# A gated delta net trunk on one core: a pair's small loads and the result stores go to GpSimd's DMA queue, and a pair waits ten steps instead of seven

## The chip, the core and the metric

The kernel runs on one core of a Trainium2 chip. The core has five engines, each with its own instruction queue: TensorE (PE in the profile, its weight loads PEld), VectorE (DVE), ScalarE (ACT), GpSimd (POOL) and SyncE (SP). A transfer between the chip's memory and the core's own memory (a DMA) is issued from the queue of one engine, in that queue's order, and runs on 16 DMA engines. The metric is the device time of one execution in microseconds, as the median of several runs.

## What is computed

A trunk of two layers over 272 tokens (16 learned ones in front of 256) of width 2048: a short convolution and a feed-forward part, then a gated delta net and a feed-forward part. The change touches the gated delta net alone:

```
proj = h @ w_in                                  # q, k (16 heads of 128), v, z (32 heads of 128), b, a
q, k, v = silu(conv4(proj[q, k, v]));  q, k = l2norm(q), l2norm(k)
beta = sigmoid(b);  g = -exp(a_log) * softplus(a + dt_bias)
# per head and chunk of tokens, g summed within the chunk:
decay = exp(g_t - g_s) for s <= t, else 0
T = inverse(I + strict(beta k k^T * decay))
u, w = T (beta v), T (beta k exp(g))
v_new = u - w S;   o = (q exp(g)) S + (q k^T * decay) v_new
S = S * exp(g_last) + (k exp(g_last - g))^T v_new
out = (rmsnorm(o) * silu(z)) @ w_out
```

## The kernel before

All arithmetic is fp32, and a weight product is made of three fp32r products: a weight is split into a high and a low part (`whi` on ScalarE, L107, `wlo` on VectorE, L108), and so are the activations; `mm3` issues the three products, L260 to L262, for each 128x128 block. Weights come in pieces of 512 KB, each by one DMA from SP's queue (L95), three pieces deep, and are split into up to four pieces ahead of use.

The gated delta net is a list of units: the gates, 16 k heads, 16 q heads, 32 z heads, then 32 v heads mixed with 128 output blocks ("o": eight stages of 16 blocks, each stage taking four finished heads). A k, q, z or v unit is 48 products over two pieces of weights; an o block is 12.

Around the units runs a clockwork. `ck.tick()` advances it: four ticks in a k, q, z or v unit and one in an o block, so that 12 weight products lie between two ticks (some o ticks and the ticks of a `drain` have none). `ck.later(n, f)` emits the instructions of `f` n ticks later, `ck.side(gen, rate)` lets a generator emit a step per tick. Since a chain of order-only dependences (`in_program_order`) keeps each engine's queue in the order in which it was emitted, a tick is a place in the program and not a time.

What the change touches:

- `k_post` (L676), `q_post` (L697), `gram` (L789) and `z_post` (L854) store the activated k, q, the Gram matrices and z to scratch in the chip's memory (`Kd`, `Qd`, `KKd`, `Zd`), from SP's queue, between the weight pieces.
- From the Gram matrices and the gates, VectorE makes the inverses of all heads at once (`inverse`), while the z units run. It leaves `Ud` and `Vd` (inverse blocks), `Md` (an off-diagonal block) and before that `Dd` (decay) in the chip's memory, all from GpSimd's queue.
- `pair(j)` works on the two value heads of key head j. It first loads `kh`, `qh` (L866, L868), then by `load` (L876), with one DMA per head: decay `D` and inverse `U` (92 partitions, 3 rows of 92 each), and the blocks `U2`, `M2`, `V2` (46 partitions, 3 rows of 46), then the gate rows `e` (L889). At step 1 it transposes k and multiplies `U2` by `M2` (L895, L900; ScalarE copies `kt` and `Y`); at step 2 `V2` by `Y` (L912) and q by k (L917); then three chunks of three steps each: `r` (L929, L932, L937), `vn` and `vd` (L941, L945, L950), the state and the output (L954 to L971). After the last chunk `tail` and `scale` normalise, load that pair's two `z` tiles (`zl`, L999) and, three ticks later, `back` transposes, multiplies by z into `y` (L1012) and splits the result (L380, L381) for the o blocks.
- `cores` paces the pairs: pair j is loaded when no other waits to start, its step 1 comes `LW` ticks later, at most two pairs are in their chunks, and each of them makes a step every two ticks.
- GpSimd's queue holds at that time the memsets of the v tiles' padding (L1099), which wait for a free buffer, and nothing else.

Of the kernel before, what the change touches and what calls it, by code (L numbers as in the profile page):

```python
# [19 lines left out]


class Dims:
    def __init__(self, D=2048, DFF=5632, NK=16, SEQ=256, META=16, C=92, FS=4, HS=4, PIECE=8, ZE=32, VA=(16, 5, 5, 4, 2, 0, 0, 0), YX=8, VB=11, GRATE=0.7, IRATE=dict(k=.3, q=.6, z=.8, v=.6, o=.6), LW=7, LIVE=2, GAP=2, RB=3, PB=4, CL=4, ZS=1, IL=6, GL=11, GY=3.0, LAG=2, X0=0, X1=4, XR=3, XP=1, FIN=3):
        self.D, self.DFF, self.NK, self.SEQ, self.META, self.C = D, DFF, NK, SEQ, META, C
        self.FS, self.HS, self.PIECE, self.ZE, self.VA, self.YX, self.VB, self.GRATE, self.IRATE = FS, HS, PIECE, ZE, VA, YX, VB, GRATE, IRATE
        self.X0, self.X1, self.XR, self.XP, self.FIN, self.LAG, self.LW, self.LIVE, self.GAP, self.RB, self.PB, self.CL = X0, X1, XR, XP, FIN, LAG, LW, LIVE, GAP, RB, PB, CL
        self.ZS, self.IL, self.GL, self.GY = ZS, IL, GL, GY
        self.T = SEQ + META
        self.KT = D // P
        self.NF = DFF // P  # L30
        self.NV = 2 * NK
        self.N = -(-self.T // C)
        self.TP = self.N * C
        self.FT = self.NF // FS
        self.NST = self.NV // HS
        kt = self.KT
        self.G4 = min(4, NK, self.KT)
        o = 0
        self.off = {}
        for name, w in (("norm", 5 * kt), ("scc", 3 * kt), ("gcc", 4 * (2 * self.NK + self.NV)),  # L40
                        ("gnw", 1), ("alog", 1), ("dtb", 1)):
            self.off[name] = o
            o += w
        self.NPAR = o
# [130 lines left out]
def trunk(ctx: ExitStack, tc: tile.TileContext, d: Dims, xT, par, w_s0, w_sc, w_sco, w_q, w_k, w_v, w_z, w_ba,  # L175
          w_go, w_gu, w_dn, outT):
    nc = tc.nc
    T, KT, NK, NV, C, N, HS = d.T, d.KT, d.NK, d.NV, d.C, d.N, d.HS
# [3 lines left out]
    TP, H = d.TP, C // 2  # L182
    PK = min(d.PIECE, KT)
    G4 = d.G4
    ck = Clockwork()
# [122 lines left out]
    class Norm:  # L308


        def __init__(self, idx, a):
            self.idx, self.a, self.n, self.wait = idx, a, 0, []
            self.acc = tp.tile([P, T], F32, tag="nacc", name="nacc", bufs=1)
# [28 lines left out]
        def finish_last(self):  # L342
# [7 lines left out]
            v = tp.tile([P, nt], F32, tag="lv", name="lv", bufs=1)  # L350
            nc.vector.tensor_scalar(out=v, in0=ps, scalar1=1.0 / d.D, scalar2=EPS, op0=ALU.mult, op1=ALU.add)
            r = tp.tile([P, nt], F32, tag="lr", name="lr", bufs=1)
# [7 lines left out]
        def finish(self):  # L360
# [4 lines left out]
            v = self.acc  # L365
            nc.vector.tensor_scalar(out=v[:, a:T], in0=ps[:, a:T], scalar1=1.0 / d.D, scalar2=EPS,
                                    op0=ALU.mult, op1=ALU.add)
# [49 lines left out]
    with tc.tile_pool(name="scy", bufs=1) as yp, tc.tile_pool(name="sct", bufs=2) as sp:  # L417
# [20 lines left out]
        for g in range(KT // G4):  # L438
            for u, ps in enumerate(pp):
# [7 lines left out]
                for i in range(G4):  # L447
                    k = g * G4 + i
# [90 lines left out]
    def dram(name, shape):  # L539
        return dp.tile(shape, F32, name=name)  # L540

    Gd, Bd, Ed, Ld = dram("Gd", [NV, TP]), dram("Bd", [NV, TP]), dram("Ed", [NV, TP]), dram("Ld", [NV, N])
    Kd, Qd = dram("Kd", [NK, P, TP]), dram("Qd", [NK, P, TP])
    Ekd, rkd, rqd = dram("Ekd", [NV, TP]), dram("rkd", [NK, TP]), dram("rqd", [NK, TP])
    KKd = dram("KKd", [NK * N, CC])
    Dd, Ud = dram("Dd", [NI, CC]), dram("Ud", [NI, CC])
    Md, Vd = dram("Md", [NI, H * H]), dram("Vd", [NI, H * H])
    Zd = dram("Zd", [NV, P, S])
# [11 lines left out]
    def psc():  # L560
        return pc_.tile([P, 512], F32, tag="c", name="psc")

    def psd():
        return pd_.tile([P, 512], F32, tag="d", name="psd")
# [104 lines left out]
    def k_post(j, ps):  # L669
        cv = conv_in(ps, vc, NK + j)  # L670
        kr = kt_.tile([P, TP], F32, tag="kr", name="kr", bufs=4)
        nc.gpsimd.memset(kr[:, T:TP], 0.0)

        def act():
            nc.scalar.activation(out=kr[:, :T], in_=cv, func=AF.Silu)
            ck.later(2, lambda: nc.sync.dma_start(out=Kd[j], in_=kr))  # L676

        ck.later(d.CL, act)
        ck.later(d.GL, lambda: gram(j, kr))
# [4 lines left out]
    def q_post(j, ps):  # L684
        if j == 0:
            state["qs"] = psd()
        qs = state["qs"]
        cv = conv_in(ps, vc, j, QA)
        qr = kt_.tile([P, TP], F32, tag="qr", name="qr")
        nc.gpsimd.memset(qr[:, :M0], 0.0)  # L690
        nc.gpsimd.memset(qr[:, T:TP], 0.0)
        sq = kt_.tile([P, T], F32, tag="sq", name="sq")

        def act():
            nc.scalar.activation(out=qr[:, M0:T], in_=cv[:, M0:T], func=AF.Silu)
            nc.scalar.activation(out=sq, in_=qr[:, :T], func=AF.Square)
            ck.later(2, lambda: nc.sync.dma_start(out=Qd[j], in_=qr))  # L697

        ck.later(d.CL, act)

        def ss():
            nc.tensor.matmul(qs[:NK, :T], onehot[:, NK - 1 - j:2 * NK - 1 - j], sq, start=(j == 0),
                             stop=(j == NK - 1))
            if j == NK - 1:
                ck.side(q_norm(qs), 1.0)

        ck.later(8, ss)
# [72 lines left out]
    def gram(j, raw):  # L780
        pk = psc()
        for n in range(N):
            kc = raw[:, n * C:(n + 1) * C]
            nc.tensor.matmul(pk[:C, n * C:(n + 1) * C], kc, kc, start=True, stop=True)
        kk = kt_.tile([C, N, C], F32, tag="kk", name="kk")
        nc.scalar.copy(out=kk.rearrange("s n c -> s (n c)"), in_=pk[:C, :N * C])

        def store():
            nc.sync.dma_start(out=KKd[j * N:(j + 1) * N].rearrange("n (s c) -> s n c", s=C), in_=kk)  # L789
            if j == NK - 1:  # L790
                ck.side(when_gates_done(), 1.0)

        ck.later(1, store)

    def when_gates_done():
        while not state.get("gdone"):
            yield 1.0
        yield from load_w()
# [51 lines left out]
    def z_post(j, ps):  # L850
        z = vc.tile([P, S], F32, tag="cx", name="z")
        nc.vector.tensor_tensor(out=z, in0=ps, in1=Rt[:, M0:T], op=ALU.mult)
        ck.later(d.ZS, lambda: nc.scalar.activation(out=z, in_=z, func=AF.Silu))
        ck.later(d.ZS + 2, lambda: nc.sync.dma_start(out=Zd[j], in_=z))  # L854


    vts = {}
# [5 lines left out]
    def pair(j, vp):  # L863
# [7 lines left out]
        def load(tag, src, a, b, bufs, r=slice(None), c=slice(None)):  # L871

            t = vp.tile([a, 2, N, b], F32, tag=tag, name=tag, bufs=bufs)
            for e in range(2):
                g = e * NK + j
                nc.sync.dma_start(out=t[:, e], in_=src[g * N:(g + 1) * N].rearrange(  # L876
                    "n (s c) -> s n c", c=(C if src.shape[1] == CC else H))[r, :, c])
            return t

        D = load("D", Dd, C, C, 3)  # L880
        U = load("U", Ud, C, C, 3)
        hi = slice(H, C)
        U2, M2, V2 = load("U2", Ud, H, H, 1, hi, hi), load("M2", Md, H, H, 1), load("V2", Vd, H, H, 1)
        qg, kg = [], []
        for x, xd in ((qg, Ed), (kg, Ekd)):
            t = vp.tile([P, 2, TP], F32, tag="e", name="e", bufs=6)
            for e in range(2):
                g = e * NK + j
# [16 lines left out]
        for x, y in ((qg, qh), (kg, kh)):  # L905
            nc.vector.tensor_tensor(out=x, in0=x, in1=y[:, None, :].to_broadcast([P, 2, TP]), op=ALU.mult)
        nc.vector.tensor_tensor(out=kd, in0=D[:, :, :, C - 1], in1=rkt[:, None, JN].to_broadcast([C, 2, N]),
                                op=ALU.mult)
        yield
        pu = psd()  # L910
        for i in range(2 * N):
            nc.tensor.matmul(pu[:H, i * H:(i + 1) * H], V2[:, i // N, i % N], Y[:, i * H:(i + 1) * H], start=True,  # L912
                             stop=True)
        nc.scalar.copy(out=U[:H, :, :, H:], in_=pu[:H, :2 * N * H].rearrange("s (e n c) -> s e n c", e=2, n=N))
        pq = psc()
# [8 lines left out]
        for n in range(N):  # L924
# [15 lines left out]
            for e in range(2):  # L940
                nc.tensor.matmul(pv[:C, e * P:(e + 1) * P], U[:, e, n], r[:, e * P:(e + 1) * P], start=True,  # L941
                                 stop=True)
# [36 lines left out]
        z = []  # L979
# [11 lines left out]
        def scale(steps, ro):  # L991
            for _ in steps:
                pass
            for i in range(2 * N):
                x = ot[:, i // N, i % N]
                nc.scalar.activation(out=x, in_=x, func=AF.Copy, scale=ro[:, i:i + 1])  # L996
            for e in range(2):
                z.append(vp.tile([P, S], F32, tag="zl", name="zl", bufs=2))
                nc.sync.dma_start(out=z[e], in_=Zd[2 * j + e])  # L999
            ck.later(3, lambda: back(0))  # L1000

        def back(e):
# [52 lines left out]
    for kind, j in gseq:  # L1055
# [8 lines left out]
        if kind == "o":  # L1064
            s, jj = divmod(j, KT)
# [17 lines left out]
        if kind == "z":  # L1083
            ps = psum(S)
            gemm(ps, xs, KT, M0, T)
            z_post(j, ps)
            ck.tick()
            continue
# [121 lines left out]
```

## Time and profile before

| | us |
|---|---|
| median of 3 runs (3059.32 to 3062.54) | 3061.09 |
| the profiled execution | 3066.19 |
| its span | 3064.4 |
| TensorE busy, share of the span | 2919.6, 95% |
| VectorE, ScalarE, GpSimd busy | 1789.2, 1368.4, 178.0 |
| mean granted clock of TensorE, share of full speed | 0.975 |
| data moved | 539.52 MB at 176 GB/s |

In the profile a wait is written as "engine line <- what released it". A row of the stretches gives, for each engine, the microseconds in which it was busy and its number of instructions, then the granted clock of TensorE as a share of full speed (its two levels are 1.2 and 2.4 GHz, so 0.5 and 1.0, and a stretch shows their mix), the busy share of the DMA engines and the rate. The units of v and o, the pairs with them, run from about 1660 to 2256 us; the gates, k, q and z before them from about 1210.

### The profile page before, as it was taken

How to read it: one execution, taken by the hardware profiler on the slowest of the kernel's cores; microseconds unless marked ns; L12 is line 12 of the kernel's file. 1: busy time of each engine (PE TensorE's matmuls, PEld its weight loads, DVE VectorE, ACT ScalarE, POOL GpSimd, SP SyncE). 2: the span in 40 equal slices, each digit the busy share in tenths (PEclk: the TensorE clock that was granted, in tenths of full speed). 3: DMA queues.
4: the chain of work that ended last, by engine and by line, in shares of the span. 5: the costliest groups of instructions: out<-in, count | busy, mean ns of one | idle time of the engine just before them, and what ended most of it. 6: DMA issues, size and time to landing. Idle time of an engine off the chain costs nothing. (4 is left out here: it accounts for less than half of the span.)

```text
span 3064.4 us, 57534 instructions
## 1 busy us (share of the span) xinstructions
PE 2919.6 (95%) x23501; PEld 2878.4 (94%) x23501; DVE 1789.2 (58%) x2628; ACT 1368.4 (45%) x2218; POOL 178.0 (6%) x306
## 2 busy tenths in 40 slices
PE   9999999999999999899998888988899999999998
PEld 8999999999999999888988788887899999999997
DVE  6555555555555557758885455555576555555555
ACT  5333444433434345745334455545454444444434
POOL 2000100000000001201000000000010000000001
PEclk9999999999999999999999899999999999999999
DMA  6555555556555565687556545444455555556564
GB/s 199 190 176 169 179 174 172 178 167 186 173 169 186 164 175 179 182 240 220 183 180 200 148 142 154 137 156 133 154 162 180 188 190 176 193 176 198 186 177 151
DMA packets 212696, 539.52 MB, mean 176 GB/s; under 512 B 55664, under 2 KB 82624, under 8 KB 211952
## 3 DMA queue, kind: packets, MB, share of 16 engines
q1 hardware_dynamic: 208144, 517.92, 54.5%
q0 software_dynamic: 2480, 15.01, 1.8%
q8 instruction: 184, 3.01, 0.4%
q10 hardware_dynamic: 1808, 2.92, 0.3%
q14 instruction: 80, 0.66, 0.1%
HBM read 515.03 MB, written 20.74 MB: 175 GB/s over the span
## 5 line engine op out<-in xcount | busy, mean ns | idle before, releaser
L108 DVE TENSOR_TENSOR wlo<-raw,whi 128x1024 fp32r<-128x1024 f32 (+2 forms) x995 | 1125.1, 1140 | 838.3 <-ACT whi L107 835.1
L262 PE MATMUL mm<-xh,wlo 128*128 128x272 f32 (+2 forms) x5136 | 1481.0, 288 | 20.9 <-DVE wlo L108 20.7
L260 PE MATMUL mm<-xh,whi 128*128 128x272 f32 (+2 forms) x5136 | 1485.4, 289 | 15.8 <-ACT whi L107 15.8
L261 PE MATMUL mm<-xl,whi 128*128 128x272 f32 (+2 forms) x5136 | 1476.3, 287 | 0.8 <-DVE xl L326 0.8
L107 ACT CAST whi<-raw 128x1024 fp32r<-128x1024 f32 (+2 forms) x995 | 962.4, 975 | 534.9 <-PE mm L261 329.9
L262 PEld LDWEIGHTS mm<-xh,wlo 128*128 128x128 f32 x5136 | 977.5, 190 | 29.1 <-DVE wlo L108 28.5
L260 PEld LDWEIGHTS mm<-xh,whi 128*128 128x128 f32 x5136 | 980.9, 191 | 25.0 <-ACT whi L107 16.8
L261 PEld LDWEIGHTS mm<-xl,whi 128*128 128x128 f32 x5136 | 978.0, 190 | 1.7 <-DVE xl L326 1.6
L262 PE MATMUL mm<-ah,wlo 128*128 128x272 f32 (+1 forms) x1408 | 399.3, 284 | 0.0
L261 PE MATMUL mm<-al,whi 128*128 128x272 f32 (+1 forms) x1408 | 399.0, 283 | 0.0
L260 PE MATMUL mm<-ah,whi 128*128 128x272 f32 (+1 forms) x1408 | 398.6, 283 | 0.0
L260 PEld LDWEIGHTS mm<-ah,whi 128*128 128x128 f32 x1408 | 265.1, 188 | 0.0
L261 PEld LDWEIGHTS mm<-al,whi 128*128 128x128 f32 x1408 | 264.6, 188 | 0.0
L262 PEld LDWEIGHTS mm<-ah,wlo 128*128 128x128 f32 x1408 | 264.3, 188 | 0.0
L380 ACT CAST ah<-u 128x272 fp32r<-128x272 f32 (+1 forms) x88 | 36.4, 413 | 286.5 <-POOL u L508 286.5
L260 PE MATMUL mm<-yh,whi 128*128 128x256 f32 x512 | 154.3, 301 | 9.3 <-DVE h L467 9.3
L261 PE MATMUL mm<-yl,whi 128*128 128x256 f32 x512 | 148.0, 289 | 0.0
L262 PE MATMUL mm<-yh,wlo 128*128 128x256 f32 x512 | 147.8, 289 | 0.0
L508 POOL TENSOR_TENSOR u<-u,g 128x272 f32<-128x272 f32 (+1 forms) x88 | 66.4, 754 | 1223.4 <-DVE u L507 1223.4
L520 ACT ACTIVATE g<-g 128x272 f32<-128x272 f32 (+1 forms) x88 | 37.3, 424 | 214.6 <-DVE g L519 214.6
L467 DVE TENSOR_TENSOR h<-mm,h 128x256 f32<-128x256 f32 (+1 forms) x272 | 113.1, 425 | 28.7 <-PE mm L262 26.4
L575 DVE SCALAR_TENSOR_TENSOR cc<-cx,prm,cc 128x271 f32<-128x271 f32 (+5 forms) x192 | 95.4, 497 | 40.0 <-ACT cc L571 35.0
(325 smaller groups left out, 2156.5 us busy)
## 6 DMA issues: line engine op xcount, KB each, us to landing
raw<-w_gu SPq DMA_DIRECT2D x352, 512.0 KB
raw<-w_dn SPq DMA_DIRECT2D x128, 384.0 KB
raw<-w_sc SPq DMA_DIRECT2D x84, 512.0 KB
raw<-w_dn SPq DMA_DIRECT2D x128, 320.0 KB
raw<-w_z SPq DMA_DIRECT2D x64, 512.0 KB
raw<-w_v SPq DMA_DIRECT2D x64, 512.0 KB
raw<-w_go SPq DMA_DIRECT2D x64, 512.0 KB
raw<-w_sco SPq DMA_DIRECT2D x32, 512.0 KB
```

Source lines behind the costliest of these rows:

```text
L107: self.nc.scalar.copy(out=hi[:, s], in_=t[:, s])
L108: self.nc.vector.tensor_tensor(out=lo[:, s], in0=t[:, s], in1=hi[:, s].bitcast(F32), op=ALU.subtract)
L260: nc.tensor.matmul(ps, wh, x[0][:, a:b], start=start, stop=False)
L261: nc.tensor.matmul(ps, wh, x[1][:, a:b], start=False, stop=False)
L262: nc.tensor.matmul(ps, wl, x[0][:, a:b], start=False, stop=stop)
L380: nc.scalar.copy(out=hi, in_=x)
L467: nc.vector.tensor_tensor(out=h[j][:, a:T], in0=ps, in1=h[j][:, a:T], op=ALU.add)
L508: nc.gpsimd.tensor_tensor(out=u1, in0=u1, in1=g1, op=ALU.mult)
L520: nc.scalar.activation(out=g1, in_=g1, func=AF.Silu)
L575: nc.vector.scalar_tensor_tensor(out=cv[:, a + i:T], in0=x1[:, a:T - i], scalar=pcol("gcc", 4 * ci + 3 - i), in1=cv[:, a + i:T], op0=ALU.m ...
```

## The change

- `load` issues from GpSimd's queue instead of SP's, so that a pair's ten loads of `D`, `U`, `U2`, `M2` and `V2` leave SP's queue; `kh`, `qh` and the gate rows `e` stay on SP.
- Those ten are put into another order: `U2`, `M2` (step 1), `D`, then `V2` and `U` (step 2).
- The stores `Kd`, `Qd`, `KKd`, `Zd` and the loads `zl` go to GpSimd's queue as well.
- `LW`, the ticks between a pair's loads and its step 1, is 10 instead of 7. It has no part in how far ahead the weights are loaded.

```diff
-... IL=..., LW=7, LIVE=2, GAP=2, ...
+... IL=..., LW=10, LIVE=2, GAP=2, ...
...
-            ck.later(2, lambda: nc.sync.dma_start(out=Kd[j], in_=kr))
+            ck.later(2, lambda: nc.gpsimd.dma_start(out=Kd[j], in_=kr))
...
-            ck.later(2, lambda: nc.sync.dma_start(out=Qd[j], in_=qr))
+            ck.later(2, lambda: nc.gpsimd.dma_start(out=Qd[j], in_=qr))
...
-            nc.sync.dma_start(out=KKd[j * N:(j + 1) * N].rearrange("n (s c) -> s n c", s=C), in_=kk)
+            nc.gpsimd.dma_start(out=KKd[j * N:(j + 1) * N].rearrange("n (s c) -> s n c", s=C), in_=kk)
...
-        ck.later(d.ZS + 2, lambda: nc.sync.dma_start(out=Zd[j], in_=z))
+        ck.later(d.ZS + 2, lambda: nc.gpsimd.dma_start(out=Zd[j], in_=z))
...
-                nc.sync.dma_start(out=t[:, e], in_=src[g * N:(g + 1) * N].rearrange(
+                nc.gpsimd.dma_start(out=t[:, e], in_=src[g * N:(g + 1) * N].rearrange(
                     "n (s c) -> s n c", c=(C if src.shape[1] == CC else H))[r, :, c])
...
+        hi = slice(H, C)
+        U2, M2 = load("U2", Ud, H, H, 1, hi, hi), load("M2", Md, H, H, 1)
         D = load("D", Dd, C, C, 3)
+        V2 = load("V2", Vd, H, H, 1)
         U = load("U", Ud, C, C, 3)
-        hi = slice(H, C)
-        U2, M2, V2 = load("U2", Ud, H, H, 1, hi, hi), load("M2", Md, H, H, 1), load("V2", Vd, H, H, 1)
...
-                nc.sync.dma_start(out=z[e], in_=Zd[2 * j + e])
+                nc.gpsimd.dma_start(out=z[e], in_=Zd[2 * j + e])
```

SP's queue at the loads of the sixth pair, among v and o units, before (`raw` is a piece of weights, `U_...`, `M_...`, `V_...` are the 46-row blocks; "x2" is one DMA for each head):

```order
L95 DMA raw_19836<-w_v 128x1024
L866 DMA kh<-Kd 128x276
L868 DMA qh<-Qd 128x276
L876 DMA D<-Dd 92x3x92 x2
L876 DMA U<-Ud 92x3x92 x2
L876 DMA U_19868<-Ud 46x3x46 x2
L876 DMA M_19871<-Md 46x3x46 x2
L876 DMA V_19874<-Vd 46x3x46 x2
L889 DMA e<-Ed 128x276 x2
L889 DMA e<-Ekd 128x276 x2
L999 DMA zl<-Zd 128x256 x2
L95 DMA raw_19938<-w_v 128x1024
```

and SP's queue at the loads of one pair in the changed kernel:

```order
L95 DMA raw_20481<-w_v 128x1024
L866 DMA kh<-Kd 128x276
L868 DMA qh<-Qd 128x276
L890 DMA e<-Ed 128x276 x2
L890 DMA e<-Ekd 128x276 x2
L95 DMA raw_20558<-w_v 128x1024
```

Eighteen DMAs between two pieces of weights have become six. GpSimd's queue among the v and o units, where before there stood the memsets alone, in the changed kernel:

```order
L1000 DMA zl<-Zd 128x256 x2
L1100 MEMSET vt 128x4
L876 DMA U_19709<-Ud 46x3x46 x2
L876 DMA M_19712<-Md 46x3x46 x2
L876 DMA D<-Dd 92x3x92 x2
L876 DMA V_19718<-Vd 46x3x46 x2
L876 DMA U<-Ud 92x3x92 x2
L1100 MEMSET vt 128x4 x2
L1000 DMA zl<-Zd 128x256 x2
```

The ten loads of a pair now stand ahead of the `zl` loads of an older pair. TensorE's queue at a pair's step 1 among o blocks, before:

```order
L262 MATMUL mm<-yh,wlo_20203 128x256
L895 MATMUL psc<-ident,kh 92x128 x2
L900 MATMUL psd<-U_20231,M_20234 46x46 x6
L968 MATMUL psc<-S,e 92x128
L969 MATMUL psc<-vn,D 92x128
L968 MATMUL psc<-S,e 92x128
L969 MATMUL psc<-vn,D 92x128
L929 MATMUL psc<-ident,vt 92x128
L932 MATMUL psc<-S,e 92x128
L929 MATMUL psc<-ident,vt 92x128
L932 MATMUL psc<-S,e 92x128
L260 MATMUL mm<-yh,whi_20293 128x256
```

and in the changed kernel, at a pair's step 1 (its lines are one higher):

```order
L262 MATMUL mm<-xh_90,wlo_20606 128x272
L896 MATMUL psc<-ident,kh 92x128 x2
L901 MATMUL psd<-U_20529,M_20532 46x46 x6
L260 MATMUL mm<-xh_92,whi_20657 128x272
L261 MATMUL mm<-xl_93,whi_20657 128x272
```

The steps of the two older pairs no longer share the tick of step 1; they stand in other ticks. Over the whole program the pairs are loaded every 10 ticks before (with longer pauses towards the end) and every 13 now, the sixteenth at the 206th instead of the 195th tick after the first v unit's start. Of the 256 ticks of v and o units the changed program has one drain: the last o stage waits for the last pair, whose `y` is emitted eight ticks after its last chunk, and only four o blocks are left to stand in between.

## Rows read from the trace of the kernel before

**Rows 1.** Busy time by stretch, us from the span's start; columns in its first row.

```profile
core 0: us, PE busy (x) PEld busy (x) DVE busy (x) ACT busy (x) POOL busy (x), PEclk, DMA share, GB/s
...
1215.00:1350.00 135.00, 124.13 (x966) 121.57 (x965) 99.07 (x142) 86.67 (x119) 19.46 (x38) 0.95 0.72 216
1350.00:1470.00 120.00, 110.18 (x819) 100.64 (x818) 84.88 (x137) 53.00 (x78) 18.39 (x60) 0.96 0.79 218
1470.00:1660.00 190.00, 168.95 (x1313) 161.02 (x1312) 145.13 (x170) 65.72 (x84) 2.35 (x14) 0.97 0.58 180
1660.00:2256.00 596.00, 520.94 (x4160) 502.89 (x4160) 332.14 (x724) 305.24 (x801) 2.29 (x26) 0.91 0.49 149
2062.00:2110.00 48.00, 45.99 (x385) 44.23 (x383) 29.05 (x68) 29.95 (x84) 0.00 (x0) 1.00 0.46 143
```

**Rows 2.** The page's chain that ended last: shares of the span, by engine, by line.

```profile
PE 34%; DMA 3%; SPq 3%; DVE 2%; ACT 2%; issue 1%; DVEq 0%; ACTq 0%
PE mm L260 10%; PE mm L262 10%; PE mm L261 10%; SPq L876 2%; DMA raw<-w_v 1%; DMA zl<-Zd 1%; SPq L889 1%; DVE wlo L108 1%; ACT whi L107 1%; PE psc L969 0%; PE psc L968 0%; PE psd L941 0%; ACT ot L996 0%; DMA raw<-w_go 0%; DVE h L467 0%
```

**Rows 3.** The same chain around one pair: start, us, what.

```profile
1806.86 3.27 DMA zl<-Zd
1810.22 0.49 DVE y L1012
...
1812.81 0.38 ACT vn L945
1813.23 1.19 PE psd L900 x12
```

**Rows 4.** SP's queue at one pair: start, us, line, DMA.

```profile
1792.41 0.38 SPq L866 DMA_DIRECT2D kh<-Kd  x1
...
1794.31 6.53 SPq L876 DMA_DIRECT2D U<-Ud  x4
...
1806.86 0.90 SPq L999 DMA_DIRECT2D zl<-Zd  x2
1807.87 0.38 SPq L95 DMA_DIRECT2D raw<-w_v  x1
```

**Rows 5.** Waits from 1660 to 2256: total us, times, longest.

```profile
ACT whi L107 <- DMA raw<-w_v: 46.2, 10, 13.2
...
DVE y L1012 <- DMA zl<-Zd: 36.4, 8, 11.1
...
PE psd L912 <- ACT Y L903: 27.5, 8, 5.5
...
PE psd L900 <- ACT vn L945: 13.1, 7, 2.0
```

**Rows 6.** GpSimd's queue from 1200 to 2300: start, us, line, DMA.

```profile
1242.61 0.58 POOL L642 DMA_DIRECT2D glb<-Ld  x1
...
1350.02 3.08 POOL L767 DMA_DIRECT2D Wt<-KKd  x6
...
1384.66 0.98 POOL L754 DMA_DIRECT2D re<-rkd  x2
```

**Rows 7.** DMA issues by line: KB each, median us from issue to landing.

```profile
wk<-Dd POOLq DMA_DIRECT2D x7, 414.0 KB, 5.8
```

**Rows 8.** Waits in the whole program: total us, times, longest.

```profile
DVE kv L742 <- DMA Wt<-KKd: 15.0, 1, 15.0
...
DVE z L852 <- DMA Zd<-z: 10.1, 1, 10.1
```

**Rows 9.** SP's own waits: total us, times, longest.

```profile
SPq L854 <- ACT z L853: 47.9, 30, 10.6
```

**Rows 10.** The chain at the last pair: start, us, what.

```profile
2247.15 0.48 ACT ot L971
...
2255.36 1.56 ACT ot L996 x5
```

**Rows 11.** The page's groups: one line's split on VectorE.

```profile
L108 DVE TENSOR_TENSOR wlo<-raw,whi 128x1024 fp32r<-128x1024 f32 (+2 forms) x995 | 1125.1, 1140 | 838.3 <-ACT whi L107 835.1
```

More of the change, by code (lines that the diff above doesn't have):

```diff
@@ L22, with __init__ @@
 class Dims:
-    def __init__(self, D=2048, DFF=5632, NK=16, SEQ=256, META=16, C=92, FS=4, HS=4, PIECE=8, ZE=32, VA=(16, 5, 5, 4, 2, 0, 0, 0), YX=8, VB=11, GRATE=0.7, IRATE=dict(k=.3, q=.6, z=.8, v=.6, o=.6), LW=7, LIVE=2, GAP=2, RB=3, PB=4, CL=4, ZS=1, IL=6, GL=11, GY=3.0, LAG=2, X0=0, X1=4, XR=3, XP=1, FIN=3):
+    def __init__(self, D=2048, DFF=5632, NK=16, SEQ=256, META=16, C=92, FS=4, HS=4, PIECE=8, ZE=32, VA=(16, 5, 5, 4, 2, 0, 0, 0), YX=8, VB=11, GRATE=0.7, IRATE=dict(k=.3, q=.6, z=.8, v=.6, o=.6), LW=10, LIVE=2, GAP=2, RB=3, PB=4, CL=4, ZS=1, IL=6, GL=11, GY=3.0, LAG=2, X0=0, X1=4, XR=3, XP=1, FIN=3):
         self.D, self.DFF, self.NK, self.SEQ, self.META, self.C = D, DFF, NK, SEQ, META, C
```

## Prediction

> **What bounds the kernel now.** I read the stretches first, to see where TensorE loses time. In the feed-forward parts it never idles; in the v and o units, 1660 to 2256, it is busy for 520.94 of 596 us at a granted clock of 0.91 [rows 1]. That is 75.1 us idle, and about 0.09 x 596 = 53.6 us of work done slowly, since the clock falls to its lower level, 1.2 GHz, after the idle spells. Together 128.7 us of 596: the same products without either would take 467.3 us. The stretch 2062 to 2110 shows what the same mix does when nothing is late: 45.99 busy of 48, clock 1.00 [rows 1], a loss of 4%. So the limit here is neither TensorE nor a busy engine (VectorE 332, ScalarE 305 of 596) but something late.
>
> Next the chain that ended last, which begins at about 1659 and so tells of this stage and the feed-forward part behind it: SP's queue holds 3% of the span and DMA 3%, some 90 us each, by line the issue of a pair's loads (L876, L889), the pieces `raw<-w_v` and `zl` [rows 2]. In order of time it shows how that comes about [rows 3]: `zl` lands 3.27 us after its issue, then `y` runs on VectorE, then ScalarE, in whose queue the split of `y` stands ahead, gets to `vn`, and then TensorE goes on at L900. SP's queue shows why `zl` was late [rows 4]: a pair's issue begins at 1792.41 with `kh`, four `U` DMAs alone take 6.53 us, `zl` leaves at 1806.86 and the next piece of weights at 1807.87. For 15.5 us no weights are issued, and `zl`, emitted one tick behind the loads, queues behind all of them. The waits count both effects: VectorE waited 36.4 us for `zl` in 8 spells, ScalarE 46.2 us for `w_v` in 10, and TensorE's own large waits, 27.5 us for `Y` and 13.1 us for `vn`, are for a ScalarE that was itself held up [rows 5].
>
> **The change part by part.** The sum is made against the profiled execution, 3066.19 us, 5.1 above the median; its span is 1.8 shorter than its own time, and I take both distances as fixed.
>
> *SP's queue.* Of 18 DMAs a pair leaves 6 there: `kh` took 0.38 us [rows 4], six such are 2.3 us. So the gap in the weights shrinks from 15.5 to about 2.5 us per pair, against two pieces per v unit and a stock of up to four split pieces. The 46.2 us of waiting for `w_v` should mostly go. What is late next on ScalarE's side is nothing that the rows show as waiting for SP.
>
> *GpSimd's queue.* It gains 12 DMAs per pair. No row shows one with 276 or 138 short pieces from this queue, so I bound it. Below: 16-row DMAs go at 0.98 / 2 = 0.49 us and 48-row ones at 3.08 / 6 = 0.51 us, and a 128-row one takes 0.58 us [rows 6]; if only the number of DMAs counts, 12 x 0.51 = 6.1 us per pair. Above: in proportion to the 128-row one, 276 pieces cost 1.25 and 138 cost 0.63 us, so 4 x 1.25 + 6 x 0.63 + 2 x 0.58 = 9.9 us. I take 8, in between, because from 16 to 128 rows the price hardly grew. Landing adds 5.8 us, the median of the `wk` loads from this queue [rows 7].
>
> *What it has time for.* The 256 ticks of the stage at 467.3 us are 1.83 us each. From the loads to step 1 there are now 10 ticks, 18.3 us; the six DMAs that step 1 needs are issued in 3 to 5 us and land by 9 to 11. From the loads of one pair to `zl` of an older one there are 8 ticks and 3 more to its use, 20.1 us; all twelve are issued and landed after 12 to 16. A pair's period is 13 ticks, 23.8 us, against 6 to 10 us of GpSimd's queue. So both arrive in time by these rows, and the cover is what `LW` = 10 adds: at 7 ticks, 12.8 us, step 1 would have 2 to 4 us to spare. The memsets ahead of the loads wait for products that stand earlier in TensorE's queue and hold nothing longer than that.
>
> *The wait of ten ticks.* Pairs come every 13 ticks instead of 10, without the later pauses, and their steps no longer share a tick. That costs nothing while o blocks are left. At the end it costs a drain: from the last chunk's `ot` copy to the last scaling of `ot` the trace has 2247.15 to 2256.9, 9.8 us [rows 10], with weight splits among it, and some 2 us of `y` and its split behind; four o blocks cover at most 4 x 1.83 = 7.3 us of that. With the slow clock behind the spell I take 6 us lost, 3 to 8.
>
> *Gates, k, q and z units.* They idle 10.9, 9.8 and 21.1 us [rows 1]. The stores leave SP, which had waited 47.9 us for the activation ahead of `Zd` [rows 9]; but in the z units VectorE is busy 145 of 190 us, no wait for `w_z` ranks among the large ones, and the weights behind those stores were in time. The last `KKd` store may land a few us earlier, and VectorE's 15.0 us wait for `Wt` shrink; the `Zd` stores now stand behind the 3 MB store `Ud` in one queue, where VectorE already waited 10.1 us for one [rows 8]. I take 0 and keep 10 us either way.
>
> *The sum.* At the clean stretch's rate the stage takes 467.3 x 48 / 45.99 = 487.7 us. To that I add 6 for the drain, 4 for the first pair, whose loads nothing has preceded, and for the 16 pairs 1.6 us each, a fifth of the 8.0 us that each loses today (128.7 / 16), since waits on VectorE and between steps remain: 26 us. That is 523.7, against 596: 72 us less. 3066.2 - 72 = 2994 for the profiled execution, 3061.1 - 72 = **2989 us** for the median. The best case, 487.7 plus 3 of drain and 10 gained before the stage, is 115 us less, 2946; with twice the remaining losses (72 us) and 10 us lost before, 3035.
>
> **The rivals.**
>
> *The engines, not the queue, make the weights late* (12%, 3025 us). A pair's pieces still pass through the same 16 DMA engines. For it: during 1660 to 2256 those are busy 0.49 of the time while TensorE waits. Against: in the z units they are busier, 0.58, without waits for weights [rows 1]. Then the `zl` half goes and the `w_v` half stays: 36 us. The Trainium skill (DMA: Bandwidth & Descriptors, "Issuing engines are not separate DMA queues") says that all queues share these engines and that issuing from several saves only issue time, usually little; here that time is 15.5 us per pair, so by that rule too the gain stands or falls with the queue.
>
> *GpSimd is held up by VectorE* (7%, 3055 us). If each of the 12 issues waits out one weight split, 1.14 us [rows 11], a pair costs 20 to 24 us of that queue, and with landing `zl` comes at 26 to 29 us instead of 20.1: late by 6 to 9 us, as much as a pair loses now, and the gain is gone but for the weights' few us. Against: six DMAs in a row went at 0.51 us each [rows 6] in a stretch where VectorE worked 85 of 120 us [rows 1]. The Trainium skill (SBUF — State Buffer, "SBUF: two separate sides") warns of this: GpSimd cannot write its descriptors while VectorE runs an operation in a two-port mode, and the remedy is to issue from SP or ACT, the opposite of this change. No row shows a stretched issue.
>
> *GpSimd's queue becomes the bound* (11%, slower, about 3124 us). With c us per issue, a pair takes 12c. The first loads come 11 ticks (20 us) into the stage, the last 54 ticks (99 us) before its end, with 15 periods between: 119 + 180c. It decides from c = 2.65 us, where that is 596; at c = 3 it is 659, 63 us slower. For it: no row has so many short pieces. Against: 0.49 to 0.58 us in all rows, a fifth of that.
>
> That the change does not do what its words say can be half granted: `LW` has no effect on weights, and GpSimd's queue does compute, though only memsets here.
>
> **How the numbers follow.** The forecast has 70%. With the first rival, faster has 82%; GpSimd held up is within 0.2% (about 6 us, what a measurement of this kernel can tell from no change) for 6 of its 7 and slower for 1; with the bound, slower has 12%. The range runs from 2955, short of the best case, to 3050, past the first rival; it leaves out the slower cases and part of the unchanged one.
>
> **What would show it.** Right: in the v and o units a granted clock of 0.96 or more and some 500 us busy of 525; no line for `y <- zl` above 10 us, `whi <- raw<-w_v` below 15; six DMAs of a pair on SP within 3 us; GpSimd's issues of `D` and `U` at 0.5 to 1.3 us; a TensorE wait of some 6 us before the last o stage. Wrong: issues on GpSimd above 2 us, or `L900 <- DMA` at every pair (its loads late); `zl` still late while issues are short (landing, not issue); SP free but `raw` late (engines).

## The result, and the profile after

The changed kernel takes 2981.31 us (median of 4 runs, 2972.83 to 2984.72) against 3061.32 us for the kernel before, beside which it was run: a ratio of 0.9735, 95% interval 0.9714 to 0.9756. The forecast of 2989 us is 8 us above it. The profiled execution takes 2980.84 us with a span of 2979.0.

All of the gain lies where it was looked for. From the last eviction of a z unit to the last product of an o block the trace has 633.7 us before (1665.2 to 2298.9) and 547.2 us after (1666.9 to 2214.1): 86.5 us less. Everything ahead of that is 1.7 us later, and the feed-forward part behind it takes 0.6 us less. The stretches of the kernel after, in the columns of [rows 1]; the fourth is its v and o units up to 2174, shortly before the last pair's last output product (2179.8) and its last `y` (2190.7):

```profile
core 0: us, PE busy (x) PEld busy (x) DVE busy (x) ACT busy (x) POOL busy (x), PEclk, DMA share, GB/s
1215.00:1350.00 135.00, 118.77 (x931) 116.75 (x930) 95.76 (x137) 84.31 (x117) 48.45 (x67) 0.95 0.70 209
1350.00:1470.00 120.00, 109.72 (x806) 99.61 (x805) 85.92 (x137) 52.10 (x77) 29.14 (x79) 0.94 0.79 221
1470.00:1660.00 190.00, 170.59 (x1337) 162.39 (x1336) 146.65 (x171) 66.51 (x85) 16.85 (x32) 0.98 0.56 181
1660.00:2174.00 514.00, 496.71 (x4221) 485.83 (x4221) 335.75 (x719) 310.92 (x794) 219.35 (x226) 0.98 0.73 177
```

TensorE is busy 496.71 of 514 us at a clock of 0.98, where it had 520.94 of 596 at 0.91. Idle time and slow clock fell together, and the DMA engines are now busy 0.73 of the time instead of 0.49. The page's chain that ended last, by engine and by line, answers to [rows 2]; SP's queue, 3% there, is down to 0%:

```profile
PE 35%; DVE 3%; ACT 3%; DMA 2%; issue 1%; SPq 0%; DVEq 0%; ACTq 0%
PE mm L260 11%; PE mm L262 11%; PE mm L261 11%; DMA raw<-w_v 2%; DVE wlo L108 1%; ACT whi L107 1%; ACT ot L997 1%; PE psc L970 1%; PE psd L942 0%; PE psc L969 0%; PE psd L955 0%; DVE h L467 0%; PE psc L918 0%; PE psd L913 0%; DMA raw<-w_go 0%
```

The waits of 1660 to 2204 (total us, times, longest) answer to [rows 5]. There is no line for `y <- zl`, where 36.4 us stood; the wait for `w_v` has fallen from 46.2 to 16.9, and TensorE's for `Y` from 27.5 to 13.7. The line on POOL is new and costs nothing: a pair's first load waits there until its buffer is free.

```profile
POOL U L876 <- PE psd L901: 237.8, 15, 20.1
...
ACT whi L107 <- DMA raw<-w_v: 16.9, 10, 4.1
...
PE psd L913 <- ACT Y L904: 13.7, 10, 2.4
...
PE psc L1011 <- ACT ot L997: 2.7, 1, 2.7
```

At one pair SP's queue now reads like this (start, us, line, DMA), to be held against [rows 4]:

```profile
1841.32 8.75 SPq L95 DMA_DIRECT2D raw<-w_v  x3
1850.17 0.57 SPq L866 DMA_DIRECT2D kh<-Kd  x1
1850.79 0.56 SPq L868 DMA_DIRECT2D qh<-Qd  x1
1851.40 1.21 SPq L890 DMA_DIRECT2D e<-Ed  x2
1852.66 1.08 SPq L890 DMA_DIRECT2D e<-Ekd  x2
1857.08 22.34 SPq L95 DMA_DIRECT2D raw<-w_go  x6
```

The six DMAs end 3.6 us after the first began; then SP has only weights to issue, and the next piece waits for its buffer until 1857.08. From `kh` to the next piece of weights it is thus 6.9 us at this pair, where [rows 4] has 15.5; the medians over the 16 pairs are 6.0 and 14.7. GpSimd's queue at the same pair:

```profile
1847.17 2.50 POOL L876 DMA_DIRECT2D U<-Ud  x2 [15.56 <-PE psd L901]
1849.67 2.44 POOL L876 DMA_DIRECT2D M<-Md  x2
1852.10 2.51 POOL L876 DMA_DIRECT2D D<-Dd  x2
1854.60 2.45 POOL L876 DMA_DIRECT2D V<-Vd  x2
1857.04 2.51 POOL L876 DMA_DIRECT2D U<-Ud  x2
...
1859.61 1.14 POOL L1000 DMA_DIRECT2D zl<-Zd  x2
```

Ten loads take 12.4 us of the queue, 1.22 to 1.26 each, whether they have 138 or 276 pieces. That is more than the upper bound of the prediction. They begin ahead of SP's `kh`, since nothing but the buffer holds them.

### The profile page after: what moved, and what is told of

Its sections match the earlier page's. It is cut to its first block, busy times and chain, and to the rows that moved or that the text cites. A ratio compares the mean times of both kernels' runs of the same rounds, so it can differ in the third digit from the quotient of the medians.

```text
span 2979.0 us, 57586 instructions
## 1 busy us (share of the span) xinstructions
PE 2888.4 (97%) x23501; PEld 2853.6 (96%) x23501; DVE 1790.8 (60%) x2628; ACT 1372.3 (46%) x2218; POOL 449.7 (15%) x578
## 5 line engine op out<-in xcount | busy, mean ns | idle before, releaser
L260 PE MATMUL mm<-xh,whi 128*128 128x272 f32 (+2 forms) x5136 | 1484.4, 289 | 14.7 <-ACT whi L107 14.7
L262 PE MATMUL mm<-xh,wlo 128*128 128x272 f32 (+2 forms) x5136 | 1479.2, 288 | 16.9 <-DVE wlo L108 16.4
L260 PEld LDWEIGHTS mm<-xh,whi 128*128 128x128 f32 x5136 | 978.5, 191 | 24.1 <-ACT whi L107 15.8
L262 PEld LDWEIGHTS mm<-xh,wlo 128*128 128x128 f32 x5136 | 975.3, 190 | 25.2 <-DVE wlo L108 24.5
L380 ACT CAST ah<-u 128x272 fp32r<-128x272 f32 (+1 forms) x88 | 36.4, 414 | 289.0 <-POOL u L508 289.0
L338 POOL TENSOR_TENSOR nacc<-nacc,nsq 128x272 f32<-128x272 f32 (+1 forms) x70 | 63.5, 907 | 621.1 <-ACT nsq L336 619.9
L467 DVE TENSOR_TENSOR h<-mm,h 128x256 f32<-128x256 f32 (+1 forms) x272 | 114.3, 425 | 26.2 <-PE mm L262 23.4
```

The lines of the kernel that those rows point to most:

```text
L260: nc.tensor.matmul(ps, wh, x[0][:, a:b], start=start, stop=False)
L262: nc.tensor.matmul(ps, wl, x[0][:, a:b], start=False, stop=stop)
L338: nc.gpsimd.tensor_tensor(out=self.acc[:, a:T], in0=self.acc[:, a:T], in1=self.sq[:, a:T], op=ALU.add)
L380: nc.scalar.copy(out=hi, in_=x)
L467: nc.vector.tensor_tensor(out=h[j][:, a:T], in0=ps, in1=h[j][:, a:T], op=ALU.add)
```

## The experiments

Two readings were open. **T**: the ten loads of a pair held up SP's queue, and with it the weights; moving them is the gain. **R1**: the gain comes from `LW` = 10, which spaces the pairs and takes `zl` away from the loads. Beside these stood the price of a load on GpSimd, and what the stores, `zl` and the order are worth.

### LW alone, loads alone

```diff
-... LW=7, ...
+... LW=10, ...        # in the kernel before
```

> The kernel before with LW = 10 as its only edit: the ten loads of a pair, zl and the stores stay on SP's queue, in the old order. Theory T (the gain comes from freeing SP's queue of the loads, so that the pieces of the v weights are no longer late): LW alone moves zl away from the loads, 8 ticks behind them and 5 ahead of the next pair's, so the wait y <- zl (36 us) should go, but SP still issues no weights for some 13 us per pair, and ScalarE's wait whi <- raw<-w_v stays at 30 to 46 us; about 3025 us (3010 to 3045). Rival R1 (the wider spacing of the pairs by LW alone makes the gain; the queue does not matter): 2981 us (2970 to 2995).

Measured: 3062.20 us against 3064.58, ratio 0.9989 (0.9980 to 0.9998). R1 has fallen. So has half of what T was given here: the wait for `zl` is gone, and the 36 us did not come back. The waits of 1660 to 2280 show where they went:

```profile
ACT whi L107 <- DMA raw<-w_v: 63.8, 13, 13.6
...
ACT whi L107 <- DMA raw<-w_go: 35.6, 7, 6.0
PE psc L932 <- DVE S L957: 34.2, 8, 7.0
```

The wait for `w_v` grew from 46.2 to 63.8 us, that for `w_go` from 13.3 to 35.6, and TensorE waited for the state `S`. The waits for `S` are the weights again, seen from another engine: at all eight of them `S` stands in VectorE's queue behind a weight split that had waited 4 to 10 us for `whi`, with at most one instruction in between, and `whi` had waited for a piece of weights. SP's queue at one pair, and VectorE's queue behind it:

```profile
1845.49 0.43 SPq L866 DMA_DIRECT2D kh<-Kd  x1
...
1847.36 6.72 SPq L876 DMA_DIRECT2D U<-Ud  x4
...
1860.34 8.41 SPq L95 DMA_DIRECT2D raw<-w_v  x4
...
1867.17 1.23 DVE L108 TENSOR_TENSOR wlo<-raw,whi 128x1024 fp32r<-128x1024 f32 x1 [8.41 <-ACT whi L107]
1868.31 0.42 DVE L957 COPY S<-psd 128x256 f32<-128x256 f32 x1
```

SP still issues no weights for 14.9 us. Over the 16 pairs these gaps add up to 228 us, against 235 in the kernel before: `LW` spaces the pairs and takes nothing out of the queue.

Whether a piece is late because it leaves late or because it travels slowly can be read in the traces. In the kernel before, eight of ScalarE's nine waits for weights from the first pair's loads on are for the first piece behind a pair's loads, with 53.6 us of the 59.5 that it waits for `w_v` and `w_go` in the stage; with `LW` = 10 there is such a wait at each of the 16 pairs. One of them, before:

```profile
1721.12 1.56 SPq L95 DMA_DIRECT2D raw<-w_v  x3
...
1726.91 1.04 ACT L107 CAST whi<-raw 128x1024 fp32r<-128x1024 f32 x1 [6.29 <-DMA raw<-w_v]
```

The eight pieces are in use 5.6 to 7.7 us after their own issue. That is no slow transfer: in after, a `w_v` piece takes 5.4 us in the median to land, and the eight that ScalarE waits for from the first pair's loads to the end of the stage take 6.4 to 11.7. What makes them late is the 14 us before their issue.

The opposite, the loads alone in the kernel before:

```diff
-                nc.sync.dma_start(out=t[:, e], in_=src[...
+                nc.gpsimd.dma_start(out=t[:, e], in_=src[...
```

> The kernel before with the ten loads of a pair on GpSimd's queue as its only edit: LW stays 7, zl and the stores stay on SP, the order is the old one. Theory T: SP's queue is free, zl is no longer behind the loads, and w_v is issued in time; step 1 comes 7 ticks (12.8 us) behind the loads, whose ten issues take 12.4 us at the 1.24 us that the trace of after shows and 5 to 9 us to land, so a few us per pair are lost at step 1 in place of the 8 of before: 3010 us (2990 to 3040). Rival R1 (spacing makes the gain): 3050 us or more, since the pairs stand as close as before.

Measured: 2983.90 us, ratio 0.9734 (0.9720 to 0.9749): the whole gain of the change, with `LW` = 7, the old order, and `zl` and the stores on SP. I had expected 3010 (2990 to 3040), so the forecast missed. Waits of 1660 to 2280: both effects are gone with the one edit, though `zl` was left where it was.

```profile
ACT whi L107 <- DMA raw<-w_v: 17.1, 8, 3.9
...
DVE y L1012 <- DMA zl<-Zd: 0.9, 1, 0.9
```

### The loads back, LW back

```diff
-                nc.gpsimd.dma_start(out=t[:, e], in_=src[...
+                nc.sync.dma_start(out=t[:, e], in_=src[...        # in the kernel after
```

> The kernel after with the ten loads of a pair back on SP's queue; LW = 10, the new order, zl and the stores on GpSimd stay. Theory T: as for LW = 10 alone, the weights are late behind the loads, the wait whi <- raw<-w_v is 30 to 46 us: about 3025 us (3010 to 3045). Rival R1: 2981 us, no change against after.

Measured: 3053.53 us, ratio 0.9963 (0.9950 to 0.9976). The direction is T's, the size is again larger than I gave it: all the rest of the change together brings 11 us, and the loads the other 70. The wait for the weights (1660 to 2280) is back and above that of before:

```profile
ACT whi L107 <- DMA raw<-w_v: 55.4, 14, 12.7
```

```diff
-... LW=10, ...
+... LW=7, ...        # in the kernel after
```

> The kernel after with LW = 7; everything on GpSimd as in after. Theory T: without the three ticks the queue's time is short twice: step 1 stands 12.8 us behind loads of which the six that it needs take 7.5 us to issue and 5 to 8 to land, and zl, emitted one tick behind the loads, queues behind all ten (12.4 us plus 8 to land) and is used 3 ticks after, so it is late by 8 to 13 us per pair, as in before: 3050 us (3020 to 3100). Rival R1 (spacing is all): the same, 3050 to 3061. A third reading, that LW does nothing and only the queue counts: 2981 us.

Measured: 2987.41 us, ratio 0.9740 (0.9723 to 0.9756), not to be told from after. My expectation of 3050 was wrong, and for the same reason as the budget in the prediction: I counted the time from a load to its use in ticks. In the records of after, a pair's first load, `U2`, is issued 27.5 us ahead of the product of step 1 that uses it (L901, median of 16 pairs), and in this kernel, three ticks shorter, still 24.1; the prediction had 18.3 and 12.8. The wait for `zl` is 1.7 us in all:

```profile
DVE y L1013 <- DMA zl<-Zd: 1.7, 1, 1.7
```

GpSimd's queue runs ahead of the engines that it serves. It has no weights to wait for, so its loads leave as soon as the buffer of the pair before is read (`U <- psd`, above), about one pair's period earlier than they are needed (the median period is 28.6 us in after and 25.2 with `LW` = 7). The place of a load in the program, which `LW` sets, is then not the time at which it is issued.

### A dose

If SP's time per pair is the cause, half of the loads should bring a part of the gain.

```diff
-                nc.sync.dma_start(out=t[:, e], in_=src[...
+                (nc.gpsimd if e else nc.sync).dma_start(out=t[:, e], in_=src[...        # in the kernel before
```

> The kernel before with half of the loads moved: of each kind the one with e = 1 goes on GpSimd's queue, the one with e = 0 stays on SP's (LW 7, the order, zl and the stores as before). A dose of the cause: SP's queue spends 13 us per pair on ten loads in before, about 6.5 here, 0 with all moved. If the loss follows the time in which SP issues no weights, half the gain of the whole move comes: 3024 us (3010 to 3035). If the split pieces in stock cover a gap of 9 us and not one of 15, nearly all of it comes: 2990 us (2982 to 3000).

Measured: 3003.44 us against 3060.55, ratio 0.9811 (0.9796 to 0.9826): 57 us, between the two forecasts. SP's queue at one pair of it:

```profile
1855.53 0.51 SPq L866 DMA_DIRECT2D kh<-Kd  x1
...
1856.95 3.40 SPq L876 DMA_DIRECT2D U<-Ud  x2
...
1865.85 0.90 SPq L999 DMA_DIRECT2D zl<-Zd  x2
1866.85 10.99 SPq L95 DMA_DIRECT2D raw<-w_v  x4
```

The stretch without weights is 11.3 us here and 15.5 in [rows 4]; the medians over the 16 pairs are 14.7 us before, 11.1 here and 5.8 with all loads moved. The first step, 3.6 us, brings 1.9% of the time, the second, 5.3 us, the last 0.8%. So the loss does not follow the gap in proportion, and the last microseconds of a gap cost most. That the pieces in stock cover the first ones is how I read it; no run changed the stock. The waits of 1664 to 2204 agree; `zl` is late again, by less:

```profile
ACT whi L107 <- DMA raw<-w_v: 20.2, 6, 7.4
DVE y L1012 <- DMA zl<-Zd: 13.0, 5, 4.5
```

### The small parts of the change

Three kernels put one part of after back each: the four stores to SP's queue, `zl` to SP's queue, the loads in the old order.

```diff
-            ck.later(2, lambda: nc.gpsimd.dma_start(out=Kd[j], in_=kr))
+            ck.later(2, lambda: nc.sync.dma_start(out=Kd[j], in_=kr))        # so Qd, KKd, Zd
...
-                nc.gpsimd.dma_start(out=z[e], in_=Zd[2 * j + e])
+                nc.sync.dma_start(out=z[e], in_=Zd[2 * j + e])
...
+        D = load("D", Dd, C, C, 3)
+        U = load("U", Ud, C, C, 3)
         U2, M2 = ...
-        D = load("D", Dd, C, C, 3)
         V2 = load("V2", Vd, H, H, 1)
-        U = load("U", Ud, C, C, 3)
```

> The kernel after with the four kinds of result stores (Kd, Qd, KKd, Zd) back on SP's queue; loads, zl and LW as in after. Theory T: the stores are worth next to nothing: KKd and Qd no longer stand behind the large stores Dd and Ud and the Wt loads in GpSimd's queue (the wait of ScalarE for KKd's store 12.9 us in after, 8.3 in before), so 0 to 6 us faster than after: 2978 us (2972 to 2985). Rival: the stores on SP hold up weights in the z units, and their move is part of the gain: 2990 us or more.

> The kernel after with only the two zl loads of a pair back on SP's queue. Theory T: SP's queue is nearly free and zl is emitted 5 ticks ahead of the next loads, so it arrives in time from either queue: 2981 us (2976 to 2988). Rival: zl on SP queues behind pieces of weights that wait for their buffers, and y waits again: 3000 to 3015 us.

> The kernel after with the loads of a pair issued in the old order (D, U, U2, M2, V2). Price theory (a load costs 1.24 us of GpSimd's queue whatever its pieces): step 1 needs D, U2 and M2, whose last issue now ends after 10 in place of 6 loads, 12.4 us in place of 7.5, and lands 5 to 8 us behind that, 17.4 to 20.4 us against the 18.3 us of ten ticks: 2981 to 2996 us, with waits of TensorE for M2 or V2 at some pairs. Rival (spacing has room to spare): 2981 us, no wait.

> The kernel after once more, unedited, on the same chip as the next three, because the variants with the stores, zl or the order put back came out 6 to 15 us below its first median. If those edits are worth something, it stands at 2981 us (2977 to 2985) again; if they were differences between chips, it comes to 2970 to 2976 us beside the others.

| kernel | us | before beside it | ratio (95%) |
|---|---|---|---|
| stores back on SP | 2971.70 | 3062.40 | 0.9706 (0.9690 to 0.9723) |
| `zl` back on SP | 2975.85 | 3062.40 | 0.9717 (0.9702 to 0.9731) |
| old order of the loads | 2974.99 | 3062.40 | 0.9714 (0.9700 to 0.9727) |
| after, unedited, once more | 2978.52 | 3060.55 | 0.9729 (0.9714 to 0.9743) |

Unedited, after stays where it was, within the first of the two forecasts, and all three intervals overlap its own. None of the three is worth anything that these runs resolve; for the stores, the ratios differ by some 7 us in favour of SP, at the edge of what they tell apart. The old order holds nothing up either: the first product of `U2` and `M2` still comes 20.2 us after a pair's last issue has ended (median of the 16 pairs), where I had feared none to spare.

### The price of a load on GpSimd

In the prediction a load's price was bounded by its pieces; after showed one price for 138 and 276. Two kernels split each load by its three chunks of rows, into three or into two.

```diff
-                nc.gpsimd.dma_start(out=t[:, e], in_=src[g * N:(g + 1) * N]...[r, :, c])
+                for n in range(N):
+                    nc.gpsimd.dma_start(out=t[:, e, n], in_=src[g * N + n]...[r, c])
```

> The kernel after with each of a pair's ten loads issued as three, one for each chunk of rows (30 issues per pair of 92 or 46 pieces each, the same bytes and pieces). If a load costs by the DMA (1.24 us each whatever its pieces), a pair takes 38 us of GpSimd's queue against a period of 23.8 us: by the sum of the rival on GpSimd's queue as the bound, 119 + 15 x 38.4 = 695 us for the v and o units, 155 us above the 540 of after: 3135 us (3080 to 3160). If it costs by the pieces or by the extent along the third axis, 30 issues take 0.4 to 0.5 us each, 12 to 15 us per pair: 2981 us (2975 to 2995).

```diff
+                for lo, up in ((0, 2), (2, N)):
+                    nc.gpsimd.dma_start(out=t[:, e, lo:up], in_=src[g * N + lo:g * N + up]...[r, :, c])
```

> The kernel after with each of a pair's ten loads issued as two, chunks 0 and 1 together and chunk 2 alone (20 per pair: of U2, M2, V2 46x2x46 with 92 pieces and 46x46 with 46; of D and U 92x2x92 with 184 and 92x92 with 92). It asks what a load of 1.24 us on GpSimd's queue costs by. If by the third axis: both 46x2x46 and 92x2x92 take about 1.2 us, the single chunks 0.5, 17 us per pair. If by more than some number of pieces between 92 and 138: 46x2x46 takes 0.5 us and 92x2x92 1.2, 13 us per pair. The time: between after and the kernel with three parts, 2967 to 2981 us, nearer to the latter if the number of packets that one load is spread over is what makes it land late.

Measured: 2966.69 us in three parts, ratio 0.9689 (0.9675 to 0.9703), and 2972.94 us in two, 0.9711 (0.9695 to 0.9727). The rows of line 876 in after, and of the same line in three and in two parts (duration in ns, least, median and largest):

```profile
L876 POOL DMA_DIRECT2D M<-Md x32: 1222/1223/1242, 1671.8 to 2113.2; - x32
L876 POOL DMA_DIRECT2D D<-Dd x32: 1255/1256/1266, 1674.3 to 2115.6; - x32
```

```profile
L877 POOL DMA_DIRECT2D M<-Md x96: 512/514/514, 1665.8 to 2093.2; - x96
L877 POOL DMA_DIRECT2D D<-Dd x96: 520/522/533, 1669.5 to 2096.7; - x96
```

```profile
L877 POOL DMA_DIRECT2D M<-Md x64: 522/838/1147, 1673.1 to 2107.8; - x64
L877 POOL DMA_DIRECT2D D<-Dd x64: 536/858/1182, 1676.4 to 2111.2; - x64
```

In two parts, half of the loads are of one chunk (the least) and half of two (the largest). A single chunk costs 0.51 to 0.54 us with 46 or 92 pieces, two chunks cost 1.14 to 1.18 us, also where `M` has only 92 pieces: the first of the two readings, 17 us of the queue per pair. So the price is not by the piece: it is about 0.5 us for a load without the axis of chunks, and 1.1 to 1.3 us for one with it. The kernel in three parts therefore spends more of GpSimd's queue (30 x 0.52 = 15.6 us per pair against 12.4), and is yet 0.4% faster than after, below both forecasts. What goes with it is that the transfers land sooner. The transfers of 1696 to 2110, of after and then in three parts (per queue: packets, MB, share of the 16 engines; per load: count, KB each, median us from issue to landing):

```profile
q1 hardware_dynamic: 25498, 60.66, 55.6%
q0 software_dynamic: 12896, 11.75, 18.8%
raw<-w_v SPq DMA_DIRECT2D x50, 512.0 KB, 5.4
e<-Ekd SPq DMA_DIRECT2D x28, 138.0 KB, 8.1
V<-Vd POOLq DMA_DIRECT2D x28, 24.8 KB, 7.6
```

```profile
q1 hardware_dynamic: 26663, 62.63, 47.2%
q0 software_dynamic: 15520, 12.03, 13.0%
raw<-w_v SPq DMA_DIRECT2D x47, 512.0 KB, 4.0
e<-Ekd SPq DMA_DIRECT2D x30, 138.0 KB, 4.8
V<-Vd POOLq DMA_DIRECT2D x90, 8.3 KB, 3.6
```

GpSimd's transfers keep the engines busy 13.0% instead of 18.8% for about the same bytes, and those of SP's queue, which were not touched, 47.2% instead of 55.6%; a weight piece lands in 4.0 us instead of 5.4, and the wait for `w_v` falls from 16.9 to 7.9 us. In two parts the piece lands in 4.3 us, the wait is 9.1, and the time lies between too. So time and landing go together; that the landing is the cause is argued, since no run changed it alone.

### Together

Loads in three parts, with stores and `zl` on SP:

> The kernel after with the loads in three parts on GpSimd's queue, and the stores and zl back on SP's queue: the single edits that came out fastest, together. If they add: 2957 us (2950 to 2963); if stores and zl were worth nothing: 2966 us as with the three parts alone (2960 to 2972); slower than that if SP's queue is again late with weights at zl, 2975 us or more.

Measured: 2967.20 us, ratio 0.9690 (0.9675 to 0.9704), the same as the three parts alone. These two are the fastest kernels here, 12 us below after by the ratios, and stores and `zl` add nothing to them.

## Why the prediction was right, and where its steps were not

- **SP's queue**: right, and more than it was given credit for. The gap of 15.5 us shrank to 3.6 us of issues against the 2.5 taken, and to 6.9 us up to the next piece of weights. The wait for `w_v` went from 46.2 to 16.9, just above the 15 that was named.
- **The price on GpSimd**: the step that failed first. 12 DMAs were put between 6.1 and 9.9 us, and took 12.4 for the ten loads and 1.1 for `zl`, 13.5 us. The upper bound scaled by pieces, and pieces have no part in it. It did no harm, since a pair has 28.6 us (median period in after; I had 23.8, with ticks of 1.83 us that last about 2.2). The issues of `D` and `U` came out at the upper bound, 1.25 us; those of the smaller blocks took 1.22 to 1.25, where 0.63 was the most that had been allowed.
- **What it has time for**: the budgets of 18.3 and 20.1 us were too small. Measured from issue to use, a pair's first load has 27.5 us and `zl` 23.4. "The cover is what `LW` = 10 adds" is refuted by the kernel with `LW` = 7, whose loads have 24.1 us.
- **The drain**: 6 us taken with the slow clock behind it, 3 to 8 named; the wait in front of the last o stage is 2.7 us (`psc L1011 <- ot`, above), where some 6 had been named as a sign. With the slow clock, 2174 to 2204 loses 4.8 us (26.94 busy of 30, at 0.94).
- **First pair**: 4 us taken; among TensorE's waits of 1660 to 2204 none is for a load.
- **Gates, k, q, z**: 0 taken, 1.7 us lost by the last z unit. The waits for the stores grew, ScalarE's for a `KKd` store, now behind `Dd`, from 8.3 to 12.9 us, and that for a `Qd` store from 5.6 to 12.6, but little of it reached TensorE.
- **The sum**: of the 128.7 us lost before it left 56.4 (523.7 - 467.3); 128.7 - 86.5 = 42.2 were left, 14 us less, and the 1.7 us lost ahead of the stage leave 13. The median came out 8 us below the forecast, the profiled execution 13 us below its 2994. That it came so near is in part luck, for two terms were off in opposite ways. 0.09 x 596 = 53.6 us counts time at the lower clock in which TensorE was idle anyway, and which stands in the 75.1 us already: of the 102.4 us at the lower clock in the trace of before, TensorE was busy for 76.9. Work done slowly thus cost about half of that, 38 us, and the floor of 467.3 us is some 15 too low. The losses put on top were too large by more: from 1660 to 2204, after is idle for 20.4 us and loses some 12 to the slow clock, 32 in place of 56.4.
- **The rival of the engines** (3025 us): fallen. The same bytes passed, at a busy share of 0.73, with weights in time, and the late pieces of before were late by their issue, not on their way (above). The engines have a smaller part: the loads in three parts, which take less of them, go with another 12 us. Its price was wrong as well: it took `zl` and the weights as halves that add, and the kernel with `LW` = 10 alone shows that the `zl` half by itself brings nothing. By the Trainium skill (DMA: Bandwidth & Descriptors, "Issuing engines are not separate DMA queues") a second queue saves only issue time, usually little; the trace agrees on what is saved, and here it is some 80 us, because ten issues stood between two weights.
- **GpSimd held up by VectorE**: no sign of it. With VectorE busy 335.75 of 514 us, all 32 issues of `M` lie between 1222 and 1242 ns. What the Trainium skill warns of (SBUF — State Buffer, "SBUF: two separate sides") is not seen in this kernel.
- **GpSimd's queue as the bound**: it decided from 2.65 us per issue; the price was 1.25. With 30 shorter issues per pair, it was still not the bound.

What stays open: why the kernel with all but the loads moved gains 11 us and the one with `LW` alone 2; and whether the stores are better on SP. The 11 us lie among the v and o units (619.7 us by the measure of 633.7 above; 632.9 with `LW` alone), so `zl` or the order is where to look, and not the stores.

## What to carry to other kernels

Look at what stands between two issues of the stream that must not be late: ten small loads among large ones cost little as transfers and 80 us as a queue. A wait that the profile shows (`zl`, and `S` with `LW` = 10) can be the same cause seen from another engine; take the cause away before adding up waits. And on a queue without weights, a load's time was set here by its buffer, so count its lead in the trace from issue to use, not in steps of the program.

## What the runs showed of the hardware that was not expected

A load from GpSimd's queue costs about 0.5 us of the queue if it is two-dimensional (46 or 92 partitions) and 1.1 to 1.3 us with an axis of chunks, two or three, independent of pieces between 92 and 276. On SP's queue, before, the median was 0.41 us for `D` and 0.72 for `V`, both with that axis.

With the same axis the load landed later, and the others with it. In the trace's records the 46-row loads with three chunks move in 6 packets of 4232 bytes each, and as single chunks in 15 packets of 552 bytes and one of 192; landing falls from 7.6 to 3.6 us for `V`. The Trainium skill (DMA: Bandwidth & Descriptors, "Why a DMA increments its semaphore by 16 and not by 1") says that a transfer is spread over as many engines, up to 16, as divide its slowest dimension on both sides, with an exception on trn2 by which some plain copies from GpSimd's queue use all 16, with a sixteenth of the partitions, rounded up, on each. Three rows per packet, 15 times and one more, is what that exception gives for 46 partitions; 23 rows per packet is what two engines would get for each chunk. The packets fit: beside the 6 of 4232 bytes each such load has 42 of 92 bytes, 48 in all, three for each of 16 engines, of which then two carry the data. The trace does not name a packet's engine, so that few engines are the reason is inferred; that the split lands sooner and leaves the engines 0.61 busy instead of 0.75 over 1696 to 2110 is measured.
